# Half a block on ScalarE's DMA queue, and eight tiny loads behind the fourth block, in a ReLU-and-sum kernel

## The chip, the cores and the metric

The kernel runs on one core of one Trainium2 chip. The metric is the device time of one execution in microseconds (us), taken as the median of several runs. A core has several engines that run side by side and meet only at semaphores. Four matter here: VectorE (DVE in the profile), ScalarE (ACT), SyncE (SP, which here only issues transfers and waits), and the 16 DMA engines that move bytes between HBM and the on-chip memory, SBUF. SBUF has 128 partitions. A transfer is issued by an instruction on some engine's own queue; in the kernel before, every transfer is issued by SP.

## The reference

The input `x` is float32 of shape 32 x 512 x 1024. Each of the 16,384 rows of 1024 numbers is clamped at zero and summed:

```python
def reference(x: np.ndarray) -> np.ndarray:
    relu_x = np.maximum(x, 0)
    return np.sum(relu_x, axis=-1).astype(np.float32)
```

67 MB are read, 64 KB are written, and each number takes part in one comparison and one addition.

## The kernel before

The rows are cut into eight blocks of 2048 rows. In a block each of the 128 partitions holds 16 rows (`ROWS = 16`), that is 64 KB which lie together in HBM, and a block is 8 MB. Seven blocks (`NB = len(TWO)`, `j` = 0 to 6) are loaded whole, by one transfer each; the last is loaded in pieces, the "tail". Three buffers (`NBUF = 3`) of a block each go round, so block `j` uses the buffer of block `j - 3`.

A block is worked on in two ways. For the counts in `TWO[j]`, ACT clamps that many rows of each partition in place with one instruction (`clamp`, L120), and DVE then sums them, all rows of that piece in one reduction (`total`, L128). For the rows counted in `ACT[j]` and `DVE[j]` one engine does both at once, one row per instruction (`act_row`, L135; `dve_row`, L143). Blocks 0 to 5 go through clamp and reduction: blocks 0, 1 and 2 as one piece of 16 rows, blocks 3 and 4 as two pieces of 8, block 5 as two of 7 with two rows for ACT alone. Block 6 is 9 rows for ACT and 7 for DVE. The tail is loads of 8 rows, of 4 rows, of two rows and a bit (`START_PIECE`), of the end of the last but one row together with the last row (`END_PIECE`), and of two pieces of 240 and 244 numbers (`PIECES`); its rows are shared between ACT and DVE, one instruction per row or piece.

The order is written out by hand; each engine runs its own instructions in program order. SP issues the loads of blocks 0, 1 and 2 at the start. From block 3 on, a load waits on SP until DVE has finished with the buffer (`freed`, the count of DVE's instructions after the block that used it). All loads leave in one queue. ACT's first instruction is the load of its function table (L118), which waits for block 0. Each block's first clamp waits for the semaphore of that block's load, and each reduction for the clamp before it. At the end SP issues three stores of the sums: block 0's, those of nearly all the other rows, and the last two columns.

Each load has a semaphore of its own (`sems.loads`), which counts 16 when the whole transfer has landed. The semaphores are cleared at the end by one instruction on SP.

Of the kernel before, what the change touches and what calls it, by code (L numbers as in the profile page):

```python
# [4 lines left out]
F32 = mybir.dt.float32  # L5
# [4 lines left out]
ROWS = 16  # L10
NBUF = 3


TWO = [[16], [16], [16], [8, 8], [8, 8], [7, 7], []]
ACT = [0, 0, 0, 0, 0, 2, 9]
DVE = [0, 0, 0, 0, 0, 0, 7]

# [2 lines left out]
TAIL = [8, 4]  # L20
START_PIECE, END_PIECE = 280, 260
PIECES = [240, 244]

EARLY = 1


def kernel(tc: tile.TileContext, x: bass.AP, out: bass.AP):
    nc = tc.nc
    sems = Semaphores(tc)

    tc.close()
    tc.compile()
    nc.cur_bb = nc.bb_map[tc.start_bb_name]
    body = nc.cur_bb.bb.instructions
    ends = list(body)
    body.clear()
    n_stores = relu_sum(nc, sems, x, out)
    body.extend(ends)


    nc.cur_bb = nc.bb_map[tc.start_bb_name + "_end"]
    nc.cur_bb.bb.instructions.clear()
    nums = sorted(s.num for s in (*sems.loads, sems.act, sems.dve))
    cleared = range(nums[0], nums[-1] + 1)
    assert len(cleared) == len(nums)
    nc.sync.sem_clear(cleared)
    nc.sync.wait_ge(sems.stored, 16 * n_stores).then_inc(sems.stored, -16 * n_stores)
    open_without_barrier(tc, EARLY)


class Semaphores:
    def __init__(self, tc: tile.TileContext):
        n = len(TWO) + len(TAIL) + 2 + len(PIECES)
        self.loads = [tc.alloc_semaphore(f"load{i}") for i in range(n)]
        self.act = tc.alloc_semaphore("act")
        self.dve = tc.alloc_semaphore("dve")
        self.stored = tc.alloc_semaphore("stored")


def relu_sum(nc, sems: Semaphores, x: bass.AP, out: bass.AP):  # L60
    x_flat = x.flatten_outer_dims()
    N, D = x_flat.shape
    NT = N // P
    NB = len(TWO)
    assert N == P * NT == P * ROWS * (NB + 1)
    assert sum(TAIL) == ROWS - 4 and START_PIECE + END_PIECE + sum(PIECES) == D

    bufs = [nc.alloc_sbuf_tensor(f"io{i}", [P, ROWS, D], F32) for i in range(NBUF)]
    res = nc.alloc_sbuf_tensor("res", [P, NT], F32)

    extra = len(PIECES) + 1
    parts = [
        nc.alloc_sbuf_tensor(f"piece{i}", [P, w + extra * (i + 1 == len(PIECES))], F32)
# [11 lines left out]
    def rows(m, n):  # L85
        if m < ROWS:
            return xf[:, m : m + n, :]
        return xv[:, m - ROWS : m - ROWS + n, :]

    def sums(m, n):  # L90
        if m < ROWS:
            return of[:, m : m + n], res[:, m : m + n]
        return ov[:, m - ROWS : m - ROWS + n], res[:, m : m + n]

    n_load = n_act = n_dve = n_store = 0

    def load(dst, src, after=None):
        nonlocal n_load
        dma = nc.sync.dma_start(out=dst, in_=src)  # L99
        if after:  # L100
            dma.wait_op(sems.dve, after[1], "sem-ge")
        dma.then_inc(sems.loads[n_load], 16)
        n_load += 1
        return sems.loads[n_load - 1]

    def store(m, n, act, dve):
        nonlocal n_store
        dst, src = sums(m, n)
        nc.sync.wait_ge(sems.act, act)
        nc.sync.dma_start(out=dst, in_=src).wait_op(sems.dve, dve, "sem-ge").then_inc(  # L110
            sems.stored, 16
        )
        n_store += 1

    def clamp(ap, loaded):
        nonlocal n_act
        if n_act == 0:
            nc.scalar.preload_act_table(RELU).wait_op(loaded, 16, "sem-ge")  # L118
            loaded = None
        i = nc.scalar.activation(out=ap, in_=ap, func=RELU)  # L120
        if loaded is not None:
            i.wait_op(loaded, 16, "sem-ge")
        i.then_inc(sems.act, 1)
        n_act += 1

    def total(ap, m, n):
        nonlocal n_dve
        nc.vector.tensor_reduce(  # L128
            out=res[:, m : m + n], in_=ap, axis=mybir.AxisListType.X, op=ADD
        ).wait_op(sems.act, n_act, "sem-ge").then_inc(sems.dve, 1)  # L130
        n_dve += 1

    def act_row(ap, accum_out, loaded):
        nonlocal n_act
        i = nc.scalar.activation(out=ap, in_=ap, func=RELU, accum_out=accum_out)  # L135
        if loaded is not None:
            i.wait_op(loaded, 16, "sem-ge")
        i.then_inc(sems.act, 1)
        n_act += 1

    def dve_row(ap, accum_out, loaded):
        nonlocal n_dve
        i = nc.vector.tensor_scalar(  # L143
            out=ap,
            in0=ap,
            scalar1=0.0,
            scalar2=None,
            op0=MAX,
            op1=ADD,
            accum_out=accum_out,  # L150
        )
        if loaded is not None:
            i.wait_op(loaded, 16, "sem-ge")
        i.then_inc(sems.dve, 1)
        n_dve += 1

    freed = []
    m = 0
    for j in range(NB):
        buf = bufs[j % NBUF]  # L160
        loaded = load(buf[:, :, :], rows(m, ROWS), j >= NBUF and freed[j - NBUF])
        c = 0
        act_waits = dve_waits = loaded
        for n in TWO[j]:
            clamp(buf[:, c : c + n, :], act_waits)
            total(buf[:, c : c + n, :], m + c, n)
            act_waits = None
            c += n
        for _ in range(ACT[j]):
            act_row(buf[:, c, :], res[:, m + c : m + c + 1], act_waits)  # L170
            act_waits = None
            c += 1
        for _ in range(DVE[j]):
            dve_row(buf[:, c, :], res[:, m + c : m + c + 1], dve_waits)
            dve_waits = None
            c += 1
        assert c == ROWS
        freed.append((n_act, n_dve))
        m += ROWS


    buf = bufs[NB % NBUF]
    c = 0
    for n in TAIL:
        loaded = load(
            buf[:, c : c + n, :], rows(m, n), None if c else freed[NB - NBUF]
        )
# [14 lines left out]
    last, w = parts[-1], PIECES[-1]  # L202
    others = [last[:, w + i : w + i + 1] for i in range(extra)]
    loaded = load(flat[:, at : at + b], src[:, :b])
# [5 lines left out]
    loaded = load(flat[:, at + end : at + 4 * D], src[:, end:])  # L210
# [7 lines left out]

    store(0, ROWS, *freed[0])
    store(ROWS, NT - ROWS - 2, sums_act, sums_dve)

    for i in range(len(PIECES) - 1):
# [3 lines left out]
        out=last[:, :],  # L228
# [12 lines left out]
def open_without_barrier(tc: tile.TileContext, n_loads: int):  # L241

    SP = mybir.EngineType.SP
    blocks = tc.nc.main_func.blocks
    opening = blocks[0].instructions
    body = next(b for b in blocks if b.name == tc.start_bb_name).instructions
    for i in list(opening):
        if isinstance(i, (mybir.InstDrain, mybir.InstEventSemaphore)):  # L250
            opening.remove(i)
    loads = [i for i in body if i.engine == SP][:n_loads]
    for i in loads:
        assert isinstance(i, mybir.InstDMACopy)
        body.remove(i)
    at = next(n for n, i in enumerate(opening) if i.engine == SP)
    opening[at:at] = loads
# [30 lines left out]
```

## Time and profile before

| What | us |
|---|---|
| median of 3 timed runs | 161.13 |
| lowest and highest of them | 160.91, 161.22 |
| span of the profiled execution, first to last instruction | 159.8 |
| median less that span (what lies around it) | 1.33 |
| DVE busy in the span | 117.6 (74%) |
| ACT busy in the span | 104.2 (65%) |
| first load landed, ACT starts | 22.05 |
| bytes moved over the span | 67.18 MB, 420 GB/s on average |

The profile is one execution, recorded by the hardware. Its own device time is not listed apart from its span; the median of the timed runs stands for it. Times are counted from the first instruction of the span. A line number such as L120 is a line of the kernel, often of a helper that several steps share. In a row of the groups the shape and the count come first, then the busy time in us and the mean of one in ns, then the idle time of the engine before those instructions and what ended it. "SPq" is the queue of transfers that SP issues. The chain that ended last goes back from the last instruction to what released it, step by step, and is printed in order of time with start, duration and what it is.

### The profile page before, as it was taken

The numbers are of one execution on the slowest core, as the hardware profiler recorded it, in microseconds if no ns is written. First come the engines' busy times: TensorE is split into PE (matmuls) and PEld (weight loads), VectorE is DVE, ScalarE is ACT, GpSimd is POOL, SyncE is SP. The second block draws the span as 40 slices with busy tenths as digits, with TensorE's granted clock in tenths as the row PEclk, the third lists the DMA queues.
The fourth block names the chain that finished last, engine by engine and source line by source line (L and its number), as shares of the span: only waits on it lengthen the run. The fifth ranks groups of instructions, "written<-read, shape, count | busy, mean of one in ns | idle before, by whom it ended". The sixth has DMA issues, their size and how long they took to land.

```text
span 159.8 us, 120 instructions
## 1 busy us (share of the span) xinstructions
DVE 117.6 (74%) x43; ACT 104.2 (65%) x50; POOL 0.2 (0%) x4
## 2 busy tenths in 40 slices
DVE  0000000006999799994999999999999999999986
ACT  0000049993699808996099951999329993499994
POOL 0000000000000000000000000000000000000000
DMA  8996996996996997999989969969969969898993
GB/s 279 508 508 279 525 508 279 525 492 295 525 492 295 525 459 328 525 394 394 525 361 426 525 295 492 525 262 525 508 279 525 508 279 525 377 410 385 425 416 102
DMA packets 2304, 67.18 MB, mean 420 GB/s; under 512 B 640, under 2 KB 896, under 8 KB 1024
## 3 DMA queue, kind: packets, MB, share of 16 engines
q1 hardware_dynamic: 2304, 67.18, 97.9%
HBM read 67.11 MB, written 0.07 MB: 420 GB/s over the span
## 4 chain that ended last, share of the span: by engine, by line
DMA 44%; DVE 33%; ACT 17%; another core or an unknown queue 3%; SPq 1%; issue 0%
DMA io<-in_x_dram 44%; DVE res L128 32%; ACT io L120 17%; SPq L99 1%; DVE io L143 0%; DVE piece L227 0%; DVE piece L143 0%
## 5 line engine op out<-in xcount | busy, mean ns | idle before, releaser
L128 DVE TENSOR_REDUCE res<-io 128x8 f32<-128x8192 f32 (+2 forms) x9 | 101.1, 11286 | 40.2 <-ACT io L120 40.2
L120 ACT ACTIVATE io<-io 128x8192 f32<-128x8192 f32 (+2 forms) x9 | 81.7, 9111 | 26.0 <-DMA io<-in_x_dram 25.9
L135 ACT ACTIVATE io<-io 128x1024 f32<-128x1024 f32 x20 | 20.9, 1044 | 6.1 <-DMA io<-in_x_dram 6.1
L143 DVE TENSOR_SCALAR_CACHE_REDUCE io<-io 128x1024 f32<-128x1024 f32 (+2 forms) x15 | 15.8, 1110 | 0.6 <-DMA io<-in_x_dram 0.4
L118 ACT ACT_TABLE_LOAD x1 | 1.3, 1283 | 22.0 <-DMA io<-in_x_dram 22.0
L135 ACT ACTIVATION_READ_ACCUMULATOR io<-io 128x1 f32 x20 | 3.7, 187 | 0.0
L143 DVE DVE_READ_ACCUMULATOR io<-io 128x1 f32 x15 | 1.2, 82 | 0.0
L227 DVE TENSOR_SCALAR_CACHE_REDUCE piece<-piece 128x247 f32<-128x247 f32 x1 | 0.4, 410 | 0.0
L143 DVE TENSOR_SCALAR_CACHE_REDUCE piece<-piece 128x240 f32<-128x240 f32 x1 | 0.4, 398 | 0.0
L272 POOL MEMSET const-bfloat16-1.0<- 128x1 bf16 x1 | 0.1, 102 | 0.0
L272 POOL MEMSET const-uint8-127<- 128x1 uint8 x1 | 0.1, 102 | 0.0
L272 POOL MEMSET const-float32-1.0<- 128x1 f32 x1 | 0.1, 99 | 0.0
L272 POOL MEMSET const-float32-0.0<- 128x1 f32 x1 | 0.1, 98 | 0.2 <-issue 0.2
L143 DVE DVE_READ_ACCUMULATOR piece<-piece 128x1 f32 x1 | 0.1, 84 | 0.0
L227 DVE DVE_READ_ACCUMULATOR piece<-piece 128x1 f32 x1 | 0.1, 83 | 0.0
## 6 DMA issues: line engine op xcount, KB each, us to landing
io<-in_x_dram SPq DMA_DIRECT2D x1, 4096.0 KB, 21.6
io<-in_x_dram SPq DMA_DIRECT2D x1, 2048.0 KB, 26.1
io<-in_x_dram SPq DMA_DIRECT2D x1, 1164.0 KB, 28.4
io<-in_x_dram SPq DMA_DIRECT2D x1, 642.0 KB, 29.6
piece<-in_x_dram SPq DMA_DIRECT2D x1, 122.0 KB, 29.2
piece<-in_x_dram SPq DMA_DIRECT2D x1, 120.0 KB, 29.4
io<-in_x_dram SPq DMA_DIRECT2D x7, 26.9
out_dram<-res SPq DMA_DIRECT2D x1, 55.0 KB, 1.6
```

What stands on the lines that cost most here:

```text
L99: dma = nc.sync.dma_start(out=dst, in_=src)
L118: nc.scalar.preload_act_table(RELU).wait_op(loaded, 16, "sem-ge")
L120: i = nc.scalar.activation(out=ap, in_=ap, func=RELU)
L128: nc.vector.tensor_reduce(out=res[:, m : m + n], in_=ap, axis=mybir.AxisListType.X, op=ADD).wait_op(sems.act, n_act, "sem-ge").then_inc(se ...
L135: i = nc.scalar.activation(out=ap, in_=ap, func=RELU, accum_out=accum_out)
L143: i = nc.vector.tensor_scalar(out=ap, in0=ap, scalar1=0.0, scalar2=None, op0=MAX, op1=ADD, accum_out=accum_out,)
L227: nc.vector.tensor_scalar(out=last[:, :], in0=last[:, :], scalar1=0.0, scalar2=None, op0=MAX, op1=ADD, accum_out=res[:, NT - 2 : NT - 1],) ...
L272: nc = _bacc.Bacc("TRN2", target_bir_lowering=False, num_devices=1)
```

## The change

Three things change.

The third block (`j = 2`) is loaded in two halves. Rows 0 to 7 of each partition come as before on SP's queue. Rows 8 to 15 are loaded by a transfer that ACT issues on its own queue, as its first instruction, once block 0 has landed. ACT waits for that half's semaphore before the third block's clamp.

The second block (`j = 1`) is clamped and summed in two pieces of 8 rows instead of one of 16.

Behind the load of the fourth block (`j = 3`) SP issues eight small loads. They copy the first 5 to 12 numbers (20 to 48 bytes) of the first 15, 14, 13, 12, 8, 4, 2 and 1 rows of `x` into a scratch tensor that nothing reads. SP waits for each of them before it issues the first store.

```diff
-TWO = [[16], [16], [16], [8, 8], [8, 8], [7, 7], []]
+TWO = [[16], [8, 8], [16], [8, 8], [8, 8], [7, 7], []]
...
+COUNTS = [15, 14, 13, 12, 8, 4, 2, 1]
...
-        n = len(TWO) + len(TAIL) + 2 + len(PIECES)
+        n = len(TWO) + len(TAIL) + 3 + len(PIECES) + len(COUNTS)
...
+    scratch = nc.alloc_sbuf_tensor("scratch", [16, 128], F32)
...
-    freed = []
+    freed, probes = [], []
     m = 0
     for j in range(NB):
         buf = bufs[j % NBUF]
-        loaded = load(buf[:, :, :], rows(m, ROWS), j >= NBUF and freed[j - NBUF])
+        if j == 2:
+            loaded = load(buf[:, :8, :], rows(m, 8))
+            half = sems.loads[n_load]
+            n_load += 1
+        else:
+            loaded = load(buf[:, :, :], rows(m, ROWS), j >= NBUF and freed[j - NBUF])
+        if j == 0:
+            nc.scalar.dma_start(out=bufs[2][:, 8:, :], in_=rows(2 * ROWS + 8, 8)).wait_op(
+                loaded, 16, "sem-ge"
+            ).then_inc(sems.loads[3], 16)
+        if j == 2:
+            nc.scalar.wait_ge(half, 16)
         c = 0
...
         freed.append((n_act, n_dve))
         m += ROWS
+        if j == 3:
+            for i, k in enumerate(COUNTS):
+                w = 5 + i
+                probes.append(load(scratch[:k, 16 * i : 16 * i + w], x_flat[:k, :w]))
...
+    for sem in probes:
+        nc.sync.wait_ge(sem, 16)
     store(0, ROWS, *freed[0])
     store(ROWS, NT - ROWS - 2, sums_act, sums_dve)
```

## The prediction

> **What bounds the kernel now.** I read the queues first, then the chain that ended last, then the groups by shape, then the timeline from block 2 to the end. Blocks are numbered from 0. The page's third and sixth parts:
>
> ```profile
> DMA packets 2304, 67.18 MB, mean 420 GB/s; under 512 B 640, under 2 KB 896, under 8 KB 1024
> q1 hardware_dynamic: 2304, 67.18, 97.9%
> ...
> io<-in_x_dram SPq DMA_DIRECT2D x7, 26.9
> ```
>
> One queue carries everything, and it is busy 97.9% of the span. A block is 128 partitions of 64 KB, so each of the 16 DMA engines moves 8 packets of 64 KB for it. The chain of waits, in order of time:
>
> ```profile
> 0.43 40.91 DMA io<-in_x_dram
> ...
> 41.37 13.86 ACT io L120
> 55.22 5.47 another core or an unknown queue
> ...
> 60.72 13.86 ACT io L120
> ...
> 74.61 51.60 DVE res L128 x5
> ...
> 127.56 29.58 DMA io<-in_x_dram
> ...
> 157.17 0.43 DVE io L143 x2
> ```
>
> Blocks 1 and 2 are clamped from 41.37 and 60.72 us, as soon as they land. In the timeline ACT starts blocks 3, 4 and 5 at 80.06, 99.42 and 118.76: a block every 19.36 us, 8.39 MB / 19.36 us = 433 GB/s, without a gap. So one 64 KB packet takes an engine 19.36 / 8 = 2.42 us, one of 32 KB 1.21. The last large transfer lands at 127.56 + 29.58 = 157.14. The kernel is bound by the stream of loads, but DVE is close behind it, as the groups by shape and the timeline show:
>
> ```profile
> L128 DVE TENSOR_REDUCE res<-io 128x16 f32<-128x16384 f32 x3 | 51.7, 17220 | 40.2 <-ACT io L120 40.2
> L120 ACT ACTIVATE io<-io 128x16384 f32<-128x16384 f32 x3 | 41.6, 13857 | 9.7 <-DMA io<-in_x_dram 9.7
> L128 DVE TENSOR_REDUCE res<-io 128x8 f32<-128x8192 f32 x4 | 34.5, 8675 | 0.0
> L143 DVE TENSOR_SCALAR_CACHE_REDUCE io<-io 128x1024 f32<-128x1024 f32 x13 | 15.0, 1214 | 0.5 <-DMA io<-in_x_dram 0.4
> ```
> ```profile
> 60.72 13.86 ACT L120 ACTIVATE io<-io 128x16384 f32<-128x16384 f32 x1 [5.49 <-DMA io<-in_x_dram]
> 74.61 66.64 DVE L128 TENSOR_REDUCE res<-io 128x16 f32<-128x16384 f32 x7 [2.13 <-ACT io L120]
> 80.06 13.95 ACT L120 ACTIVATE io<-io 128x8192 f32<-128x8192 f32 x2 [5.49 <-DMA io<-in_x_dram]
> ...
> 155.53 1.22 DVE L143 TENSOR_SCALAR_CACHE_REDUCE io<-io 128x1024 f32<-128x1024 f32 x1 [0.44 <-DMA io<-in_x_dram]
> ...
> 157.17 0.42 DVE L143 TENSOR_SCALAR_CACHE_REDUCE io<-io 128x260 f32<-128x260 f32 x1
> ```
>
> From 74.61 DVE never waits until the last rows: seven reductions without a gap, and single rows from 141.17. Between there and the end it idles 0.08 us at 152.64, 0.44 at 155.09 and 0.05 at 157.12. Hence the number that decides here: **DVE has 0.57 us to spare after block 2's clamp.** Whatever starts block 2's reduction later than 74.61 + 0.57 = 75.18 moves the end by the excess.
>
> **What it is measured against.** The profiled execution's span is 159.8 us; the three timed runs have a median of 161.13 (160.91 to 161.22), 1.33 above it for what lies around the span. I add the sum to 161.13. About 0.2%, 0.3 us, is what a measurement of this kernel can tell from no change.
>
> **The change part by part.** *The half block on ScalarE's queue.* The issue waits for block 0 (22.05). Behind it on ACT stand the table load and every clamp, which waited for the same landing before. New is the issue itself: SP's take 0.33 to 0.45 us (L99's row), so I take 0.4. Block 0's clamp ends at 37.6 instead of 37.20 and its reduction at 54.9 instead of 54.45. The load of block 3 then leaves 0.4 later, at 54.9; the queue needs it about 2.3 us before 60.7 (the first load: 22.05 landed, less 0.38 of issue, less 8 x 2.42), so by 58.4. All hidden; without that cover 0.4 us.
>
> What is not hidden is what the half meets. At 22.4 block 1 is in flight on SP's queue, on the same 16 engines. The half is 4.19 MB, 19.36 / 2 = 9.68 us of the stream, wanted only at 60.7, and whatever of it goes ahead of block 1's end makes block 1 late. The trace of before has one queue and doesn't show two share. Bounds: none of the half goes first, and block 1 lands at 41.34 as now; or all of it, 41.34 + 9.68 = 51.0. A gain is excluded: the same bytes go through a stream without gaps. I take turns packet by packet: the packet records have every 64 KB row as a packet of its own, one after the other on an engine. Block 1's first packets start at 20.9 to 21.7 in them and last to 23.3 to 24.1; the half's are ready some 0.6 to 1.5 us after their issue, as the first load's were (1.0 to 1.9 us, after an issue that ended at 0.38), at 23.0 to 23.9. So they join after block 1's first or second packet, and seven or six of their eight lie ahead of its eighth. Seven: 41.34 + 7 x 1.21 = 49.8. Six give 48.6, all eight (or equal shares by bytes) 51.0.
>
> The Trainium skill ("DMA: Bandwidth & Descriptors", "Queues, rings and completion order") says that each engine takes its queues in turn, a whole packet at a time, and that a packet is typically 9 to 17 descriptors. No run here shows which descriptors form one; the records above have one a row. If a load's 8 rows an engine were one packet, block 1 would be done before the switch, and the sum would be 0 instead of 2.5.
>
> Then, on ACT: 49.8 + 0.03 + 13.95 (two clamps of 8 rows) + 0.02 + 13.86 (block 2's clamp) + 0.03 = 77.69. Block 2's other half is complete at 60.7 as before, since the bytes ahead of it are the same, and ScalarE's half lands before that; the added wait for it, with block 2's clamp behind it, is over long before 63.8. Block 2's reduction starts at 77.69 instead of 74.61: 3.08 late. All that DVE does after it follows without a gap, so it ends 3.08 - 0.57 = **2.5 us** later. With 48.6 it is 1.3, with 51.0 3.7.
>
> *Block 1 in two clamps.* 13.95 instead of 13.86 on ACT, counted above. DVE starts on the first half at 49.8 + 7.05 = 56.9 and is done at 56.9 + 17.27 = 74.1, before 77.69, so DVE waits 3.6 us there and the split saves nothing at the end. Uncut, block 1's reduction would run 63.7 to 80.9 and hold up block 2's by 3.2 more: that is what the split is worth here.
>
> *Later loads.* Buffers come free at 74.1 (was 72.47), 94.9 (91.83), 112.2 (109.0) and 129.3 (126.2). With 2.3 us of lead the queue needs them by 77.8, 97.1, 116.5 and 135.8. No gap; the least room is 2.2 us.
>
> *The eight small loads.* They go on SP's queue behind block 3. Their issue: 8 x 0.33 to 0.45 = 2.6 to 3.6 us, from 55.3 to 58.9, while SP would wait for 74.1 anyhow. On the DMA engines nothing so small is loaded before. From above: the two piece loads of 120 and 122 KB land some 0.3 us apart, so 8 x 0.3 = 2.4; from below: the stores' packets of 8 bytes last 9 ns, those of 64 bytes 11, and two an engine and load (data and semaphore) make 16 x 0.01 = 0.16. I take 0.16, as the nearer size. Either is hidden: with DVE 2.5 late, all loads behind could come up to 2.5 later. Without that cover it would be 0.16, at most 2.4.
>
> *Their waits.* Eight waits on SP stand ahead of the first store, which now leaves at 129.11 and would at some 132; they were satisfied 70 us before, and the next store has to wait until 156.8. Nothing. The final store (1.4 us to landing) and the clearing of nine more semaphores lie behind DVE's end as before.
>
> Sum: 161.13 + 2.5 = 163.6.
>
> **The rivals.** *Not slower: block 1 goes first.* If the engines finish what SP's queue has begun, block 1 lands at 41.4, its clamps run to 55.3, its reductions from 54.9 to 72.2, block 2's starts at 74.6, and the time is 161.1 to 161.3. It decides from a landing of block 1 before 75.18 - 27.9 = 47.3, that is with at most 4 of the half's 8 packets ahead. For it: block 1 was issued 21 us earlier and its packets stand ready. Against it: nothing in the trace puts one queue over another. *All the half first, or equal shares:* 51.0, so 161.13 + 3.7 = 164.8. For it: halves the size at equal bytes end before block 1 does. *Two queues move fewer bytes:* the windows from 154 to 156 us, with smaller packets, moved 406 GB/s instead of 433, 6% less; over the 29 us of sharing that is 1.8 us, block 1 lands at 51.6 and the time is 161.13 + 4.88 - 0.57 = 165.4. Against it: the packets stay at 32 and 64 KB. *The small loads hold the queue,* each for the 1.4 us that the 1 KB store takes to land: 8 x 1.4 = 11 us, some 172. Against it are the 0.3 us between two piece loads.
>
> The page cited above also says, in "Issuing engines are not separate DMA queues", that transfers begun on several engines interleave on the same 16 and only the issue time is saved. No run here shows it yet; by it the first rival falls.
>
> **How the numbers follow.** Turns with six or seven packets ahead 0.50 (162.4 to 163.6); all the half first 0.25 (164.8); fewer bytes 0.08 (165.4); small loads hold 0.02; block 1 first 0.11 (161.1 to 161.3); something that shortens the end and that I don't see 0.04. The range runs from 161.2 to 165.3: left out are half of block 1 first, the gain, the small loads and half of fewer bytes. Slower by over 0.2%: 0.85; within: 0.11; faster: 0.04.
>
> **What would show it.** ACT's first clamp of block 1 starts near 49.8 instead of 41.37, block 2's near 63.8 with no wait for DMA before it; block 2's reduction near 77.7, after 3.6 us of idle DVE; the rows from 144 on without DVE waiting for DMA; the last chain running through DVE from 77.7 to the end, not through DMA; blocks 3 to 6 still at 80.1, 99.4, 118.8 and 138.1 (within 0.2). A clamp of block 1 before 47.3 would make the prediction wrong, as would a block 3 over 2.5 us late, or a gap in DVE after 77.7.

## The result, and the profile after

The changed kernel takes 163.28 us (163.23 to 163.33), the kernel before, beside it, 161.09: a ratio of 1.0137, 95% interval 1.0124 to 1.0149. The forecast was 163.6, slower. The profiled execution took 163.23 us with a span of 161.9, against 159.8 before.

The page's third part now has two queues; q10 is ScalarE's, and it carries half a block:

```profile
DMA packets 2586, 67.18 MB, mean 415 GB/s; under 512 B 794, under 2 KB 1050, under 8 KB 1178
q1 hardware_dynamic: 2442, 62.98, 90.9%
q10 hardware_dynamic: 144, 4.19, 6.0%
```

The chain that ended last, in order of time (start, duration, what):

```profile
0.43 49.29 DMA io<-in_x_dram
...
49.75 2.44 ACT io L122
52.19 4.50 issue
56.68 20.77 ACT io L122 x2
...
77.47 66.65 DVE res L130 x7
144.12 14.02 DVE io L145 x25
158.14 0.71 issue
158.85 0.80 DVE io L145 x5
...
```

Before, it ended in a DMA of 29.58 us and a landing at 157.14. Now its last DMA is the one that brings block 1, at 49.72; from there it goes through ACT's three clamps and then through DVE to the end. The end is no longer set by the last loads. The 4.50 us of "issue" are the rest of the first clamp, since the timeline below has ACT busy without a stop there. The 0.71 us of "issue" lies inside a run of single rows which start 1.14 us apart before and after it; no wait for a load stands there. The timeline has the same events with the waits before them (start, busy, engine, line, what, idle before and its releaser):

```profile
21.90 0.38 ACTq L170 DMA_DIRECT2D io<-in_x_dram  x1
...
49.75 27.70 ACT L122 ACTIVATE io<-io 128x8192 f32<-128x8192 f32 x3 [12.28 <-DMA io<-in_x_dram]
...
56.81 17.28 DVE L130 TENSOR_REDUCE res<-io 128x8 f32<-128x8192 f32 x2 [2.09 <-ACT io L122]
...
77.47 66.65 DVE L130 TENSOR_REDUCE res<-io 128x16 f32<-128x16384 f32 x7 [3.39 <-ACT io L122]
80.04 13.95 ACT L122 ACTIVATE io<-io 128x8192 f32<-128x8192 f32 x2 [2.60 <-DMA io<-in_x_dram]
99.76 13.95 ACT L122 ACTIVATE io<-io 128x8192 f32<-128x8192 f32 x2 [5.77 <-DMA io<-in_x_dram]
```

ACT waits 12.28 us for block 1 (4.17 before), then runs three clamps without a stop. DVE waits 3.39 us for the third of them, block 2's, and starts block 2's reduction at 77.47 instead of 74.61.

The packet records show why block 1 came late. They don't name the engine, but each packet starts where another ended, and so they fall into 16 sequences, one for each engine. One of them between 21 and 54 us, S for SP's queue and A for ScalarE's, with the start in us and the size (4 B is the packet that raises the semaphore):

```
S20.96:4B S20.96:64K S23.38:64K A25.80:32K S27.01:64K A29.42:32K S30.63:64K A33.05:32K
S34.26:64K A36.67:32K S37.88:64K A40.29:32K S41.50:64K A43.92:32K S45.12:64K A47.54:32K
S48.75:4B A48.76:32K S49.96:32K A51.17:4B S51.18:32K S52.39:32K
```

Block 1's third to eighth packets each have one packet of ScalarE's before them, and so has its semaphore packet: seven turns of 1.21 us. The other 15 show the same order.

### The profile page after: what moved, and what is told of

Read it like the earlier page. It is cut to its first block, busy times and chain, and to the rows that moved or that the text cites. A ratio compares the mean times of both kernels' runs of the same rounds, so it can differ in the third digit from the quotient of the medians.

```text
span 161.9 us, 136 instructions
## 1 busy us (share of the span) xinstructions
DVE 117.4 (73%) x44; ACT 104.2 (64%) x51; POOL 0.2 (0%) x4
## 4 chain that ended last, share of the span: by engine, by line
DVE 51%; DMA 30%; ACT 14%; issue 3%; SPq 0%
DVE res L130 41%; DMA io<-in_x_dram 30%; ACT io L122 14%; DVE io L145 9%; DVE piece L246 0%; SPq L101 0%; DVE piece L145 0%
```

## The experiments

The theory: the two queues take turns on each engine, one packet at a time; so the half delays block 1 and with it block 2's clamp and reduction; and DVE, which has under 1 us to spare, carries the delay to the end. The small loads and the cut of block 1 play no part in the loss. The rivals are the small loads, sharing by bytes, a lasting cost of a second queue, and a loss in the stream itself. All ratios are to the kernel before, run on the same chip beside each.

**One part taken out.** `no_half` loads block 2 whole on SP's queue again:

```diff
...
-        if j == 2:
-            loaded = load(buf[:, :8, :], rows(m, 8))
...
-        else:
-            loaded = load(buf[:, :, :], rows(m, ROWS), j >= NBUF and freed[j - NBUF])
...
+        loaded = load(buf[:, :, :], rows(m, ROWS), j >= NBUF and freed[j - NBUF])
```

> The eight small loads and the cut of block 1 in two stay; block 2 comes whole on SP's queue again. Theory (ScalarE's half takes turns with block 1, packet by packet, and makes it late): block 1 lands near 41.3, block 2's reduction starts at 74.6, DVE waits for loads at the end again, and the time is 161.1 plus what the small loads cost the stream, 0.3 by the landing of block 4 after the change (99.74 instead of 99.42): 161.4. Rival (the small loads are what costs): 163.3 as after the change.

Measured: 161.41 us, ratio 1.0021 (1.0010 to 1.0032). Its chain is that of the kernel before again:

```profile
74.55 51.60 DVE res L130 x5
...
127.50 30.07 DMA io<-in_x_dram
```

So the half is nearly the whole loss. The 0.3 us left are in the loads: block 4 lands at 99.81.

`no_small` leaves the half and takes the small loads out:

```diff
-COUNTS = [15, 14, 13, 12, 8, 4, 2, 1]
+COUNTS = []
```

> The half on ScalarE's queue and the cut of block 1 stay; the eight small loads and their waits go. Theory: block 1 still lands at 49.7, block 2's reduction still starts at 77.5, and the time stays at 163.3, since DVE sets the end and hides the 0.3 us of the small loads. Rival (small loads): 161.1.

Measured: 163.23 us, ratio 1.013 (1.011 to 1.015). Block 4 lands at 99.33, 0.4 earlier than after the change, and the time is the same: with DVE late, what the small loads cost the stream is hidden. The two parts don't add up: 0.3 alone, nothing beside the half.

**Other sizes of packet.** `twelve_rows` puts twelve rows on ScalarE's queue, in packets of 48 KB:

```diff
-            loaded = load(buf[:, :8, :], rows(m, 8))
+            loaded = load(buf[:, :4, :], rows(m, 4))
...
-            nc.scalar.dma_start(out=bufs[2][:, 8:, :], in_=rows(2 * ROWS + 8, 8)).wait_op(
+            nc.scalar.dma_start(out=bufs[2][:, 4:, :], in_=rows(2 * ROWS + 4, 12)).wait_op(
```

> Twelve of the 16 rows of block 2 come on ScalarE's queue instead of eight: packets of 48 KB. Theory (turns): seven turns of 1.82 us, block 1 lands at 41.2 + 12.7 = 53.9, block 2's reduction starts 27.7 later, at 81.6; DVE has 0.8 us to spare after 74.6, so it ends 6.2 later: 167.3. Rival (shares by bytes or all of it first): 41.2 + 14.5 = 55.7, and 169.1. Rival (bandwidth lost while two queues are open): block 2 complete later than 60.7, too.

Measured: 167.52 us, ratio 1.0394 (1.0373 to 1.0414). Its timeline:

```profile
53.84 41.54 ACT L122 ACTIVATE io<-io 128x8192 f32<-128x8192 f32 x5 [16.47 <-DMA io<-in_x_dram]
...
81.56 25.81 DVE L130 TENSOR_REDUCE res<-io 128x16 f32<-128x16384 f32 x2 [3.39 <-ACT io L122]
```

Block 1 is clamped from 53.84 and block 2 reduced from 81.56, where turns by packet gave 53.9 and 81.6. Sharing by bytes, 55.7, falls. Block 2 is complete at 60.53, no later than before (60.70), so no bandwidth was lost while two queues were open.

`two_of_four` sends the same half in packets of 16 KB:

```diff
...
-            nc.scalar.dma_start(out=bufs[2][:, 8:, :], in_=rows(2 * ROWS + 8, 8)).wait_op(
-                loaded, 16, "sem-ge"
-            ).then_inc(sems.loads[3], 16)
+            nc.scalar.dma_start(
+                out=bufs[2][:, 8:12, :], in_=rows(2 * ROWS + 8, 4)
+            ).wait_op(loaded, 16, "sem-ge").then_inc(sems.loads[3], 16)
+            nc.scalar.dma_start(
+                out=bufs[2][:, 12:, :], in_=rows(2 * ROWS + 12, 4)
+            ).then_inc(sems.loads[4], 16)
...
```

> The same half of block 2 at the same moment on the same queue, but as two transfers of four rows, so in packets of 16 KB instead of 32. Theory (one packet from each queue in turn): seven turns of 0.61 us, block 1 lands at 41.2 + 4.3 = 45.5, its clamps end at 59.5, before block 2 is complete at 60.7, block 2's reduction starts at 74.6, and the time is 161.4. Rival (the queues share by bytes, or the half goes first): block 1 lands at 50.9, block 2's reduction starts at 78.6, and the time is 161.1 + 3.2 = 164.3 or, if it is as after the change, 163.3.

Measured: 163.17 us, ratio 1.0122 (1.0103 to 1.0141): the theory's time was missed by 1.8 us. Its landing of block 1 was not. The timeline, then the piece of the chain that ends with the landing of the second transfer:

```profile
45.63 13.95 ACT L122 ACTIVATE io<-io 128x8192 f32<-128x8192 f32 x2 [7.56 <-DMA io<-in_x_dram]
...
63.35 13.86 ACT L122 ACTIVATE io<-io 128x16384 f32<-128x16384 f32 x1 [3.77 <-DMA io<-in_x_dram]
...
77.23 25.81 DVE L130 TENSOR_REDUCE res<-io 128x16 f32<-128x16384 f32 x2 [4.73 <-ACT io L122]
```
```profile
22.43 40.80 DMA io<-in_x_dram
```

Block 1 arrives at 45.6, as turns of 0.61 us make it. But the second transfer's semaphore is full only at 22.43 + 40.80 = 63.23, so block 2's clamp starts 2.6 us later than before. The packet records of one engine, put together as above, show what it waited for:

```
S57.24:32K A58.45:16K S59.05:4B A59.06:16K S59.66:64K A62.08:4B S62.09:64K
```

ScalarE's last data packet is over at 59.66, but its semaphore packet has to wait for a turn too, and that turn belongs to block 3's first packet, 2.42 us long. The other 15 engines show the same. In the changed kernel ScalarE's queue was empty by 51.8, and nothing of block 3 stood against it. The expectation had left out that block 3's load stands on SP's queue by then.

`four_rows` tests that with one transfer of four rows on ScalarE's queue, the other twelve on SP's, so that ScalarE's queue is done early (by 47.7 us in its packet records). `four_rows_no_small` is the same without the small loads.

```diff
-            loaded = load(buf[:, :8, :], rows(m, 8))
+            loaded = load(buf[:, :12, :], rows(m, 12))
...
-            nc.scalar.dma_start(out=bufs[2][:, 8:, :], in_=rows(2 * ROWS + 8, 8)).wait_op(
+            nc.scalar.dma_start(out=bufs[2][:, 12:, :], in_=rows(2 * ROWS + 12, 4)).wait_op(
```

> One transfer of four rows (packets of 16 KB) on ScalarE's queue instead of eight; SP loads the other 12 rows of block 2. The small loads and the cut of block 1 stay. Theory (turns, semaphore packets included): block 1 lands at 41.2 + 7 x 0.61 = 45.5 as in the run with two transfers, but ScalarE's queue is done by 48, long before block 3's first packet, so its semaphore waits for no packet of 64 KB; block 2 is complete at 60.6, its reduction starts at 74.5, and the time is 161.4 (0.3 for the small loads). Rival (a transfer on the second queue costs some 2 us by itself): 163.2.

> The same without the eight small loads. Theory: nothing of the change that reaches the end is left: 161.1, as before. Rival (second queue): 163.2.

Measured: 161.47 us, ratio 1.0024 (1.0014 to 1.0034), and 161.14 us, ratio 1.0005 (0.9995 to 1.0014). The timeline of `four_rows`:

```profile
45.68 13.95 ACT L122 ACTIVATE io<-io 128x8192 f32<-128x8192 f32 x2 [8.04 <-DMA io<-in_x_dram]
...
60.82 13.86 ACT L122 ACTIVATE io<-io 128x16384 f32<-128x16384 f32 x1 [1.19 <-DMA io<-in_x_dram]
...
74.71 25.81 DVE L130 TENSOR_REDUCE res<-io 128x16 f32<-128x16384 f32 x2 [2.63 <-ACT io L122]
```

Block 1 is as late as in `two_of_four`, block 2 is in time, and the loss is gone. Block 1 may be 4.3 us late for nothing, and a transfer on the second queue costs nothing here by itself.

**DVE's part.** `third_split` gives DVE block 2 in two pieces, so that it needn't wait for a clamp of 16 rows; `second_whole` takes block 1's cut back:

```diff
-TWO = [[16], [8, 8], [16], [8, 8], [8, 8], [7, 7], []]
+TWO = [[16], [8, 8], [8, 8], [8, 8], [8, 8], [7, 7], []]
```
```diff
-TWO = [[16], [8, 8], [16], [8, 8], [8, 8], [7, 7], []]
+TWO = [[16], [16], [16], [8, 8], [8, 8], [7, 7], []]
```

> The changed kernel, with block 2 clamped and summed in two pieces of 8 rows, too. Theory (what costs is DVE's wait from 74.1 to 77.5 for block 2's clamp): the first piece is clamped by 63.7 + 7.0 = 70.7, DVE goes from block 1's reduction at 74.1 straight on, is done with block 2 at 91.4 (before the change 91.83), and the end is set by the loads again: 161.1 + 0.3 for the small loads = 161.4. Rival (the loss lies in the loads, not in DVE): 163.3 as after the change.

> The changed kernel, with block 1 in one piece of 16 rows as before. Theory: its clamp ends at 49.7 + 13.9 = 63.6, its reduction at 80.8, block 2's starts there instead of 77.5, 3.3 later, and so does the end: 166.6. If the cut of block 1 does nothing: 163.3.

Measured: `third_split` 161.66 us, ratio 1.0040 (1.0025 to 1.0055); `second_whole` 166.43 us, ratio 1.034 (1.0325 to 1.0355). The chain of `third_split`:

```profile
49.74 7.04 ACT io L122
...
56.81 68.85 DVE res L130 x8
...
126.52 29.13 DMA io<-in_x_dram
```

and of `second_whole`:

```profile
49.69 13.87 ACT io L122
...
63.58 83.77 DVE res L130 x8
```

With block 1 just as late (49.7), splitting block 2's work takes away the 3.39 us of waiting, and the end goes back to the loads: the loss was DVE's wait, not lost bytes. The run is 0.26 above the forecast 161.4, and its profile (span 160.0, less than `no_half`'s 160.3) doesn't say why; the intervals of the two runs overlap. `second_whole` shows that the cut of block 1 saved 3.2 us of what the half would have cost.

**The small loads by themselves.** Block 2 comes whole, as in `no_half`, and the list changes:

```diff
-COUNTS = [15, 14, 13, 12, 8, 4, 2, 1]
+COUNTS = [1]
+COUNTS = [16]
+COUNTS = [16] * 4
+COUNTS = [16] * 8
```

(one line for each of `one_small`, `one_sixteen`, `four_sixteens` and `sixteens`).

> Block 2 whole on SP's queue, and of the eight small loads one, for one partition (20 bytes on one DMA engine). The end is set by the loads, so the time shows what small loads cost the stream. If the cost is that of their packets (9 to 11 ns each): 161.1. If the first large packet behind any small one is longer, whatever the count: 161.2 to 161.4, when the engine that gets it is the slowest, less if it isn't.

> Block 2 whole on SP's queue, one small load of 16 partitions, so that every DMA engine gets two small packets behind block 3. If the stream loses time to each small packet beyond its own 9 ns: 0.94 / 8 = 0.12 late, 161.15. If the large packet behind is longer only after many small ones: 161.05, every first packet of block 4 at 2.42 us. If a single small load on each engine is enough for it: 161.6 to 162.0.

> Block 2 whole on SP's queue, four small loads of 16 partitions, eight small packets on every engine. In proportion to eight such loads (0.94): 161.5. If it only begins with more small packets than these: 161.1 to 161.2 (8 x 0.01 us for the packets themselves).

> Block 2 whole on SP's queue, and eight small loads of 16 partitions each, so that every DMA engine gets 16 small packets (eight of data, eight of semaphores). If the cost is that of the packets: 16 x 0.01 = 0.16, 161.3, and block 4 lands at 99.6. If the large packet behind them is longer as after the change (up to 3.2 us instead of 2.42): block 4 lands 0.5 to 0.9 late, and the time is 161.6 to 162.0.

Measured, with the duration of the 16 packets of 64 KB that came first after them, one on each engine (before the change block 4 lands at 99.40):

| Run | us, ratio (interval) | block 4 lands | first packets, us |
|---|---|---|---|
| `one_small` | 161.06, 1.0003 (0.9993 to 1.0012) | 99.30 | 2.42 |
| `one_sixteen` | 161.11, 0.9998 (0.9989 to 1.0008) | 99.17 | 2.42 |
| `four_sixteens` | 161.13, 1.0004 (0.9994 to 1.0014) | 99.32 | 2.42 to 2.55 |
| `no_half` (15 down to 1) | 161.41, 1.0021 (1.0010 to 1.0032) | 99.81 | 2.42 to 3.07 |
| `sixteens` | 161.97, 1.0060 (1.0043 to 1.0076) | 100.34 | 2.50 to 3.30 |

The timeline of `sixteens` has ACT's clamp of block 4, which started at 99.42 before:

```profile
100.36 7.03 ACT L122 ACTIVATE io<-io 128x8192 f32<-128x8192 f32 x1 [6.55 <-DMA io<-in_x_dram]
```

The small packets themselves last 7 to 11 ns. Part of the cost lies in the large packet behind them, and it isn't in proportion: four loads on every engine cost nothing that can be measured, eight 0.94 us. In `sixteens` the small packets also take longer to pass. From the end of an engine's last packet of block 3 to the start of its first of block 4 there are 0.38 us on average, against 0.05 in `four_sixteens`.

That gap tells how many small loads an engine had: 2 to 3 ns in `no_small`, 14 with one load on every engine, 49 to 50 with four. `four_rows` has the list of the change. If a load of k partitions runs on the same first k engines, its 16 gaps, from 2 to 101 ns in steps of 11 to 13 for each load, can be matched to the counts in one way only:

| Small loads on the engine | Engines | first packet, us |
|---|---|---|
| none to four | 8 | 2.42 to 2.43 |
| five | 4 | 2.69 to 2.77 |
| six | 2 | 2.79, 2.81 |
| seven | 1 | 2.89 |
| eight | 1 | 3.11 |

After the change, too, eight of the 16 first packets are above 2.6 us. Loads five to eight are those of 36 bytes and more: whether the number or the size decides wasn't tried.

A long first packet isn't special to small loads. The 16 that open the kernel before, with nothing ahead of them, took 2.43 to 3.43 us. In `second_whole`, where block 4's load left only at 80.83, as the small ones were landing, 14 of the 16 were above 2.6. Whether small loads cost what a queue that has run dry costs is not shown; no run here separates the two.

## Why the prediction was right, step by step

**The decisive number** was right in kind and short in size. DVE was said to have 0.57 us to spare, counted from the ends of its accumulator reads, the short instructions that fetch a row's sum. But where DVE isn't held up, the next row starts beside that read, 1.14 us after the one before. The timeline of before:

```profile
151.43 0.08 DVE L143 DVE_READ_ACCUMULATOR io<-io 128x1 f32 x1
151.43 1.21 DVE L143 TENSOR_SCALAR_CACHE_REDUCE io<-io 128x1024 f32<-128x1024 f32 x1
...
152.56 0.08 DVE L143 DVE_READ_ACCUMULATOR io<-io 128x1 f32 x1
152.72 1.22 DVE L143 TENSOR_SCALAR_CACHE_REDUCE io<-io 128x1024 f32<-128x1024 f32 x1
...
155.01 0.08 DVE L143 DVE_READ_ACCUMULATOR io<-io 128x1 f32 x1
...
157.04 0.08 DVE L143 DVE_READ_ACCUMULATOR io<-io 128x1 f32 x1
```

So its idle time was 152.72 - 152.56, 155.53 - 155.01 and 157.17 - 157.04: 0.81. After the change all of it is used up: block 2's reduction is 77.47 - 74.61 = 2.86 late, and 2.86 - 0.81 = 2.05; DVE's last instruction ends at 160.42 instead of 158.38, 2.04 late. The timed runs differ by 2.19.

**Block 1's landing** was put at 49.8 and came at 49.73, by seven turns. The mechanism is the one forecast, but the count was lucky. The forecast left open whether the half joins after block 1's first packet (seven ahead of its eighth) or its second (six, a landing at 48.6 and a time of 162.4), and took seven without a reason. On every engine the half joined after the second: six packets lie ahead of block 1's eighth, and the seventh ahead of its semaphore packet, which the forecast had not given a turn. The two slips cancel; each alone would have put the landing 1.2 us off.

**ACT's chain** was 27.9 from landing to block 2's reduction and measured 27.7: three clamps in a row take 27.70 by the timeline, not 13.95 + 13.86 and gaps. With the 0.24 of spare time and the 0.1 of block 1's landing, that is the difference between 2.5 and 2.04.

**What was costed at nothing** stayed hidden. The issue on ACT took 0.38 (0.4 was taken). DVE's wait after block 1 was 3.39, not 3.6. The first forecast block landing that missed is block 4's: 99.74 instead of 99.4, outside the 0.2 that were named, and 119.08 and 138.44 follow it. The small loads were put at 0.16 and cost 0.3 by `no_half`. The cover named for them, up to 2.5 us, held, and `no_small` shows that they change nothing here. Their waits were said to be satisfied 70 us before the first store. The small loads stand behind block 3 and the last lands at 81.19, so it was 51; that still costs nothing.

**The rivals.** Block 1 first, all the half first and sharing by bytes are excluded by the packet records and by `twelve_rows`; fewer bytes by block 2's landing at 60.64 (60.70 before); small loads that hold the queue by `no_small`. The threshold of the first rival, block 1 landing before 47.3, was not reached by the change; `four_rows`, with block 1 at 45.7, is on its other side and loses nothing but the 0.3 us. The time alone would not have decided: the range took in "all the half first" (164.8) as well, and it is the landing of block 1 that tells the two apart.

**What a turn is.** The Trainium skill ("DMA: Bandwidth & Descriptors", "Queues, rings and completion order") has an engine change queues only after a packet, and calls 9 to 17 descriptors a packet typical. The turns are there, but here each row of 16 to 64 KB, and each semaphore write, was a turn of its own; if a load's eight rows an engine were one turn, block 1 would have landed at 41.3, and it landed at 49.7. Where they differ, the measurement decides. Its section "Issuing engines are not separate DMA queues" agrees: the half interleaved on the same 16 engines, and three blocks were complete at 60.64 as before.

## What to carry to other kernels

The stream of loads was already full here, and a transfer on a second queue brought nothing sooner in total; it moved its own bytes ahead of others. Ask which load it delays, by turns of its packet size, and how long the engine that waits for that load can wait. And count the spare time of the second-busiest engine from where instructions start, since an operation that overlaps the next one, as the accumulator reads do here, doesn't use it up.

## What was not expected of the hardware

A transfer's semaphore packet takes a turn like any other. In `two_of_four` it came 2.42 us after the last of its data, behind one packet of 64 KB of a later block on the other queue. So a transfer can land late by a large packet of another queue, though its own packets (16 KB there) are small.

Small loads in a row cost more than their packets: four on every engine nothing, eight 0.94 us, of which the packets are some 16 x 0.01 = 0.16. The rest lies in the time that they take to pass (0.38 us on average, these 0.16 with it) and in the first large packet behind them (2.50 to 3.30 us instead of 2.42). Why is not settled.
